# The first load of a streaming log-sum-exp, cut into four transfers of strided partitions ahead of the opening barrier

## The chip, the cores and the metric

The kernel runs on one core of one Trainium2 chip. The metric is the device time of one execution in microseconds (us), the median of several runs; less is better. All runs compared here were at a granted clock of 1.0. Differences below about 0.2% are within the noise unless an interval is given.

## The reference, cut to what matters

```
x: float32, 32 x 512 x 1024, standard normal
x_max = max(x, axis=-1)
out   = x_max + log(sum(exp(x - x_max), axis=-1))      # 32 x 512 values
```

The input is 64 MiB and is read once. The kernel leaves out the maximum, which these inputs don't need.

## The kernel before

Each of the 128 SBUF partitions owns 128 consecutive rows of the input. A row is 1024 float32 values, 4 KB, so the rows of neighbouring partitions lie 512 KB apart in memory. The rows come in 17 loads ("chunks") into a ring of 51 row slots. ScalarE (ACT) takes the exponentials in place; the sums are taken by VectorE (DVE) for some rows and by ACT's own accumulator for the others.

```python
CHUNKS = [(4, 1), (15, 11), (16, 10), (16, 15), (16, 0), (14, 0), ...]   # (rows, rows summed on DVE)
RING_ROWS = 51
FIRST_PARTS = [("sync", 0, 128)]
# ... cut ...
x_v = x_flat.rearrange("(p t) d -> p t d", p=P)

def load(i):
    (s, row), r = place[i], CHUNKS[i][0]
    # ... waits until the slots are free ...
    for engine, lo, hi in FIRST_PARTS if i == 0 else [("sync", 0, P)]:
        getattr(nc, engine).dma_start(
            out=ring[lo:hi, s : s + r], in_=x_v[lo:hi, row : row + r]
        ).then_inc(landed[i], 16)
# ... cut ...
load(0)
n_early = len(body.instructions)          # these go ahead of the opening barrier
# ... cut: for each chunk, load(i), then
nc.scalar.wait_ge(landed[i], 16 * (len(FIRST_PARTS) if i == 0 else 1))
# exp on ACT, sums on DVE or ACT ...
# ... cut: at the end the first n_early instructions are moved in front of
# the drain with which SyncE enters the opening barrier ...
```

So the first load, four rows for each partition (128 pieces of 16 KB, 2 MB), is issued by SyncE as its very first instruction (at 0.00 us), and the second load only after the barrier (at 0.78 us).

The softmax here doesn't subtract the row's maximum and nothing guards it: scores larger than these inputs give would overflow.

Of the kernel before, what the change touches and what calls it, by code (L numbers as in the profile page):

```python
# [1 line left out]

# [4 lines left out]



CHUNKS = [  # L10
    (4, 1), (15, 11), (16, 10), (16, 15), (16, 0), (14, 0), (12, 9), (9, 5), (7, 5), (5, 4),
    (4, 3), (3, 0), (2, 2), (2, 2), (1, 0), (1, 0), (1, 0),
]
RING_ROWS = 51

LN_AT = 5

FIRST_PARTS = [("sync", 0, 128)]


@with_exitstack
def kernel(
    ctx: ExitStack,
    tc: tile.TileContext,
    x: bass.AP,
    axis: bass.AP,
    out: bass.AP,
):
    nc = tc.nc
    P = nc.NUM_PARTITIONS  # L30

    assert axis in (-1, len(x.shape) - 1), f"only last-axis reduction supported, got {axis}"

    x_flat = x.flatten_outer_dims()
    N, D = x_flat.shape
    assert N % P == 0
    NB = N // P
    assert sum(r for r, _ in CHUNKS) == NB

    fp32 = mybir.dt.float32  # L40
    Exp = mybir.ActivationFunctionType.Exp
    Ln = mybir.ActivationFunctionType.Ln
    AX = mybir.AxisListType.X

    x_v = x_flat.rearrange("(p t) d -> p t d", p=P)
    out_v = bass.AP(tensor=out.tensor, offset=out.offset, ap=[[NB, P], [1, NB]])

    ring = nc.alloc_sbuf_tensor("ring", [P, RING_ROWS, D], fp32).ap()
    sums = nc.alloc_sbuf_tensor("sums", [P, NB], fp32).ap()
    res = nc.alloc_sbuf_tensor("res", [P, NB], fp32).ap()  # L50

    landed = [tc.alloc_semaphore(f"landed{i}") for i in range(len(CHUNKS))]
    act_done = tc.alloc_semaphore("act_done")
    dve_done = tc.alloc_semaphore("dve_done")
    stored = tc.alloc_semaphore("stored")


    hook = nc.pop_inst_callback()
    symbolic, nc._always_lower_symbolic_ap = nc._always_lower_symbolic_ap, False


    place = []
    row = slot = 0
    for r, _ in CHUNKS:
        if slot + r > RING_ROWS:
            slot = 0
        place.append((slot, row))
        slot += r
        row += r



    busy = [(0, 0)] * RING_ROWS
    acts = dves = 0

    def load(i):
        (s, row), r = place[i], CHUNKS[i][0]
        act_wait = max(a for a, _ in busy[s : s + r])
        dve_wait = max(d for _, d in busy[s : s + r])
        if dve_wait:  # L80
            nc.sync.wait_ge(dve_done, dve_wait)
        if act_wait:
            nc.sync.wait_ge(act_done, act_wait)
        for engine, lo, hi in FIRST_PARTS if i == 0 else [("sync", 0, P)]:
            getattr(nc, engine).dma_start(
                out=ring[lo:hi, s : s + r], in_=x_v[lo:hi, row : row + r]
            ).then_inc(landed[i], 16)

    def take_logs(lo, hi, dve_wait, act_wait):
        nonlocal acts  # L90
        nc.scalar.wait_ge(act_done, act_wait)
        nc.scalar.wait_ge(dve_done, dve_wait)
        nc.scalar.activation(out=res[:, lo:hi], in_=sums[:, lo:hi], func=Ln).then_inc(  # L93
            act_done, 1
        )
        acts += 1

    body = nc.main_func.blocks[-1]
    assert not body.instructions
    load(0)  # L100
    n_early = len(body.instructions)

    nc.scalar.preload_act_table_set("natural_log_exp_and_others")  # L103

    logged = 0
    done_before = [(0, 0)]
    for i, (r, n_dve) in enumerate(CHUNKS):
        if i:
            load(i)
        s, row = place[i]  # L110
        if i == LN_AT:
            logged = row
            take_logs(0, logged, *done_before[i])
        nc.scalar.wait_ge(landed[i], 16 * (len(FIRST_PARTS) if i == 0 else 1))
        if n_dve:
            nc.scalar.activation(  # L116
                out=ring[:, s : s + n_dve], in_=ring[:, s : s + n_dve], func=Exp
            ).then_inc(act_done, 1)
            acts += 1
            nc.vector.wait_ge(act_done, acts)  # L120
            nc.vector.reduce_sum(  # L121
                out=sums[:, row : row + n_dve], in_=ring[:, s : s + n_dve], axis=AX
            ).then_inc(dve_done, 1)
            dves += 1
            for j in range(n_dve):
                busy[s + j] = (0, dves)
        for j in range(n_dve, r):
            nc.scalar.activation(  # L128
                out=ring[:, s + j],
                in_=ring[:, s + j],  # L130
                func=Exp,
                accum_out=sums[:, row + j : row + j + 1],
            ).then_inc(act_done, 1)
            acts += 1
            busy[s + j] = (acts, 0)
        done_before.append((dves, acts))

    take_logs(logged, NB, dves, acts)
    nc.scalar.wait_ge(act_done, acts)
    nc.scalar.dma_start(out=out_v, in_=res).then_inc(stored, 16)  # L140
    nc.gpsimd.wait_ge(stored, 16)



    first = nc.main_func.blocks[0]
    head, work = first.instructions, body.instructions
    end = next(k for k, i in enumerate(head) if i.opcode == "UnconditionalBranch")
    head, tail = head[:end], head[end:]
    for ins in work[:n_early]:
        at = next(  # L150
            k for k, i in enumerate(head) if i.engine == ins.engine and i.opcode == "Drain"
        )
        head.insert(at, ins)
    first.instructions = head + work[n_early:] + tail
    body.instructions = []

    nc._always_lower_symbolic_ap = symbolic
    nc.push_inst_callback(hook)


# [1 line left out]
_INS = ['x', 'axis']  # L162
_OUTS = [((32, 512), 'float32')]

_NUMBERS = {'axis': -1}


# [26 lines left out]
```

## Time and profile before

| | before |
|---|---|
| median time | 164.12 us (164.01 to 164.53, 6 runs) |
| span of the profiled execution | 162.2 us |
| ACT first waits for data until | 7.42 us |
| second load awaited until | 25.62 us |
| fifth load awaited until | 83.69 us |

The profiled execution took 163.96 us, a little less than all six timed ones.

The following lines are the chain of waits of the kernel before: start in us, duration in us, what. It follows the work that ended last back from the end.

```profile
31 pieces in order of time: start us, us, what
0.71 0.07 issue
0.78 24.82 DMA ring<-in_x_dram
...
25.62 9.60 ACT ring L116
...
35.24 11.90 DVE sums L121
...
47.15 36.52 DMA ring<-in_x_dram
...
83.69 10.55 ACT ring L128 x21
...
159.36 0.25 ACT res L93
```

These are lines of its timeline: start, duration, engine, line, operation, operands, count, and in brackets how long the engine had been idle and what ended that.

```profile
0.00 2.38 SPq L85 DMA_DIRECT2D ring<-in_x_dram  x4
0.77 1.28 ACT L103 ACT_TABLE_LOAD   x1 [0.77 <-PEq L175]
7.42 1.06 ACT L116 ACTIVATE ring<-ring 128x1024 f32<-128x1024 f32 x1 [5.37 <-DMA ring<-in_x_dram]
25.62 9.59 ACT L116 ACTIVATE ring<-ring 128x11264 f32<-128x11264 f32 x1 [14.02 <-DMA ring<-in_x_dram]
44.98 8.74 ACT L116 ACTIVATE ring<-ring 128x10240 f32<-128x10240 f32 x1 [5.62 <-DMA ring<-in_x_dram]
83.69 1.06 ACT L128 ACTIVATE ring<-ring 128x1024 f32<-128x1024 f32 x1 [5.29 <-DMA ring<-in_x_dram]
```

Read together they say this. Up to 83.69 us ACT repeatedly waits for data; after it the chain stays with ACT. The chain names ACT and DVE between 25.6 and 47.2 us, because the issue of the fifth load waited for slots. But the records of single packets in the trace show that the engines were still moving the fourth load until about 64 us. The stream never stopped (the engines' mean busy share is 1.01 from 47 to 64 us, at 439 GB/s, and 0.97 from 64 to 83.6 us, at 421), so the landing at 83.67 us is plain transfer time. In this kernel, then, what delays the start of the stream should delay the end by as much.

The last view is the table of windows: window, its length, then for each engine its busy time and (number of instructions), the clock, the mean busy share of the 16 DMA engines, and GB/s.

```profile
core 0: us, DVE busy (x) ACT busy (x) POOL busy (x), PEclk, DMA share, GB/s
0.00:3.00 3.00, 0.00 (x0) 1.28 (x1) 0.20 (x4) 1.00 0.59 208
3.00:6.00 3.00, 0.00 (x0) 0.00 (x0) 0.00 (x0) 1.00 1.03 437
```

From 3 us on the first load runs at 437 GB/s, about what the loads after it reach (438 GB/s from 12 to 28 us). In the packet records each engine moves a 16 KB piece every 607 ns (27.0 GB/s).

### The profile page before, as it was taken

Reading aid. Unit: us, or ns where it says so; the run is one execution under the profiler, and the core shown is the slowest. Engines: PE = TensorE matmul, PEld = TensorE weight load, DVE = VectorE, ACT = ScalarE, POOL = GpSimd, SP = SyncE. Lnnn points to the kernel's source line nnn. Section 1 sums busy time; section 2 is a strip of 40 time slices with the busy share of each in tenths; the row PEclk is TensorE's granted clock in tenths of the full one; section 3 lists DMA queues with packets and bytes.
Section 4 is the critical chain, followed back from the end, with each engine's and each line's share of the span. In section 5 each row is a group of like instructions: output and inputs, shape, how many; then the busy total and the mean of one; then the engine's idle time right before and its main releaser. Section 6 shows DMA issues by size and latency. Waiting matters only on the chain.

```text
span 162.2 us, 213 instructions
## 1 busy us (share of the span) xinstructions
DVE 72.9 (45%) x11; ACT 124.1 (76%) x136; POOL 0.2 (0%) x4
## 2 busy tenths in 40 slices
DVE  0030000039960799000999900000006999799591
ACT  3180006997099971999339999999999999999993
POOL 0000000000000000000000000000000000000000
DMA  6999899969969959969988999999999999999970
GB/s 263 497 485 470 349 394 517 485 291 517 485 291 517 517 259 517 517 275 501 517 368 370 424 424 432 461 497 388 436 427 399 431 400 439 420 424 414 415 318 16
DMA packets 2593, 67.18 MB, mean 414 GB/s; under 512 B 288, under 2 KB 416, under 8 KB 800
## 3 DMA queue, kind: packets, MB, share of 16 engines
q1 hardware_dynamic: 2448, 67.11, 96.4%
q10 hardware_dynamic: 144, 0.07, 0.1%
q14 instruction: 1, 0.01, 0.0%
HBM read 67.11 MB, written 0.07 MB: 414 GB/s over the span
## 4 chain that ended last, share of the span: by engine, by line
ACT 52%; DMA 38%; DVE 7%; issue 1%
DMA ring<-in_x_dram 38%; ACT ring L128 30%; ACT ring L116 22%; DVE sums L121 7%; ACT res L93 0%
## 5 line engine op out<-in xcount | busy, mean ns | idle before, releaser
L121 DVE TENSOR_REDUCE sums<-ring 128x5 f32<-128x5120 f32 (+8 forms) x11 | 72.9, 6648 | 86.0 <-ACT ring L116 85.9
L116 ACT ACTIVATE ring<-ring 128x5120 f32<-128x5120 f32 (+8 forms) x11 | 59.3, 5394 | 29.4 <-DMA ring<-in_x_dram 29.4
L128 ACT ACTIVATE ring<-ring 128x1024 f32<-128x1024 f32 x61 | 63.4, 1041 | 5.3 <-DMA ring<-in_x_dram 5.3
L128 ACT ACTIVATION_READ_ACCUMULATOR ring<-ring 128x1 f32 x61 | 11.4, 187 | 0.0
L103 ACT ACT_TABLE_LOAD x1 | 1.3, 1283 | 0.8 <-PEq L175 0.8
L93 ACT ACTIVATE res<-sums 128x67 f32<-128x67 f32 (+1 forms) x2 | 0.5, 256 | 0.1
L175 POOL MEMSET const-bfloat16-1.0<- 128x1 bf16 x1 | 0.1, 101 | 0.0
L175 POOL MEMSET const-uint8-127<- 128x1 uint8 x1 | 0.1, 101 | 0.0
L175 POOL MEMSET const-float32-0.0<- 128x1 f32 x1 | 0.1, 98 | 0.2 <-issue 0.2
L175 POOL MEMSET const-float32-1.0<- 128x1 f32 x1 | 0.1, 98 | 0.0
## 6 DMA issues: line engine op xcount, KB each, us to landing
ring<-in_x_dram SPq DMA_DIRECT2D x1, 7680.0 KB, 24.8
ring<-in_x_dram SPq DMA_DIRECT2D x1, 7168.0 KB, 36.1
ring<-in_x_dram SPq DMA_DIRECT2D x1, 6144.0 KB, 21.6
ring<-in_x_dram SPq DMA_DIRECT2D x1, 4608.0 KB, 32.1
ring<-in_x_dram SPq DMA_DIRECT2D x2, 2048.0 KB, 26.3
ring<-in_x_dram SPq DMA_DIRECT2D x1, 3584.0 KB, 40.2
ring<-in_x_dram SPq DMA_DIRECT2D x1, 2560.0 KB, 44.4
ring<-in_x_dram SPq DMA_DIRECT2D x2, 1024.0 KB, 46.0
```

The lines of the kernel that those rows point to most:

```text
L93: nc.scalar.activation(out=res[:, lo:hi], in_=sums[:, lo:hi], func=Ln).then_inc(act_done, 1)
L103: nc.scalar.preload_act_table_set("natural_log_exp_and_others")
L116: nc.scalar.activation(out=ring[:, s : s + n_dve], in_=ring[:, s : s + n_dve], func=Exp).then_inc(act_done, 1)
L121: nc.vector.reduce_sum(out=sums[:, row : row + n_dve], in_=ring[:, s : s + n_dve], axis=AX).then_inc(dve_done, 1)
L128: nc.scalar.activation(out=ring[:, s + j], in_=ring[:, s + j], func=Exp, accum_out=sums[:, row + j : row + j + 1],).then_inc(act_done, 1)
L175: nc = _bacc.Bacc("TRN2", target_bir_lowering=False, num_devices=1)
```

## The change

The intent is to get the engines going earlier. The first load becomes four transfers of 16, 16, 32 and 64 partitions, taken in strides: on average one, one, two and four pieces for each of the 16 engines. The author hoped that the engines would start earlier on a first transfer of only 16 pieces. All four are issued ahead of the opening barrier.

```diff
-FIRST_PARTS = [("sync", 0, 128)]
+FIRST_PARTS = [(0, 8), (4, 8), (2, 4), (1, 2)]
...
-        for engine, lo, hi in FIRST_PARTS if i == 0 else [("sync", 0, P)]:
-            getattr(nc, engine).dma_start(
-                out=ring[lo:hi, s : s + r], in_=x_v[lo:hi, row : row + r]
+        for lo, step in FIRST_PARTS if i == 0 else [(0, 1)]:
+            nc.sync.dma_start(
+                out=ring[lo:P:step, s : s + r], in_=x_v[lo:P:step, row : row + r]
             ).then_inc(landed[i], 16)
```

## The prediction

> **What bounds the kernel now.** Until 83.67 us it is the stream of loads: the timeline and the chain of waits have the first load awaited until 7.42 us, the second until 25.62, the fifth until 83.67. The chain names a slot wait at 47.15, but the packet records show the engines still fed then (the fourth load drains at about 64 us), so the landing at 83.67 is pure transfer. From there to 159.6 us ScalarE (ACT) works almost without a gap. So what the first load gains or loses reaches the fifth landing and moves the end as much.
>
> **The first load now.** The timeline has its issue at 0.0 (372 ns on the queue). In the packet records the first packets start from 1.08 us, spread over almost 0.9 us among the 16 engines. Then each engine moves one 16 KB row every 607 ns (27.0 GB/s) without gaps; the eight rows end at 6.42 to 7.04 us, and that stagger of 0.6 us stays in every later load. The final store of 128 small rows spread its engines by only some 0.15 us[...].
>
> **What the change does.** The same 128 rows of 16 KB, in transfers of 16, 16, 32 and 64 rows. Added: three issues of about 330 to 370 ns on SyncE and 48 completion packets (9 ns each, three per engine). The later parts are issued at about 0.37, 0.7 and 1.05 us, before the engines finish the rows ahead, so no starvation. The opening barrier ends about 1.05 us later: the table load moves from 0.77 to 1.8 us, still long before the data; the second load is issued at about 1.8 instead of 0.78, with 5 us of packets ahead of it. Nothing lost there.
>
> Gain: [...] I estimate 0.1 to 0.4 us, from the two spreads above.
>
> [...]
>
> Weights: [...] first two parts only, about 165 (0.25); nearly all parts, 167 to 168.8 (0.4).
>
> **Prediction.** 165.2 us, range 163.7 to 168.6. Faster by over 2%: 0.01; within 2%: 0.68; slower: 0.31.
>
> **What would show it.** [...] The fifth landing moves from 83.67 by as much; ACT stays gapless after it. SyncE's four issues take about 0.35 us each before the barrier.
>
> **What would make it wrong.** [...] a completion write that stalls an engine between parts; a fixed cost per transfer above the 0.6 us of a row, which would starve the engines; a later load recovering a loss.

The danger was the assumption that, depending on the partitions which a transfer writes, a piece might take about 1.2 us, twice the 607 ns measured. Against the gain of 0.1 to 0.4 us the sum then had three cases: no piece slower, 163.6 to 164.2 us (weight 0.35); slow pieces in the first two parts, +1.2 us, about 165; slow pieces in nearly all parts, up to +4.9 us (0.6 us more for each of eight pieces) less what the stagger resolves, 167 to 168.8. The first load was to be awaited until about 7.1, 8.3 and up to 12 us. The point of 165.2 us and its range weigh all three cases.

## The result, and the profile after

| | before | after |
|---|---|---|
| median time, 6 runs each | 164.12 us (164.01 to 164.53) | 166.22 us (166.01 to 167.08) |
| ratio | | 1.0131, 95% interval 1.0109 to 1.0153 |
| first load awaited until | 7.42 us | 9.93 us |
| second load awaited until | 25.62 us | 28.07 us |
| fifth load awaited until | 83.69 us | 86.14 us |

A ratio here and below is the mean time of one kernel's runs over that of the other's in the same rounds, so it is not quite the ratio of the medians that are quoted.

The change costs 2.1 us, 1.3%: slower, clear of the noise, and within 2%. Lines of the timeline of the kernel after (columns as above):

```profile
0.00 4.99 SPq L85 DMA_DIRECT2D ring<-in_x_dram  x7
3.14 1.28 ACT L103 ACT_TABLE_LOAD   x1 [3.14 <-PEq L175]
9.93 1.06 ACT L116 ACTIVATE ring<-ring 128x1024 f32<-128x1024 f32 x1 [5.50 <-DMA ring<-in_x_dram]
28.07 9.59 ACT L116 ACTIVATE ring<-ring 128x11264 f32<-128x11264 f32 x1 [13.97 <-DMA ring<-in_x_dram]
47.42 8.74 ACT L116 ACTIVATE ring<-ring 128x10240 f32<-128x10240 f32 x1 [5.60 <-DMA ring<-in_x_dram]
86.14 1.06 ACT L128 ACTIVATE ring<-ring 128x1024 f32<-128x1024 f32 x1 [5.32 <-DMA ring<-in_x_dram]
103.76 1.06 ACT L128 ACTIVATE ring<-ring 128x1024 f32<-128x1024 f32 x1 [0.60 <-DMA ring<-in_x_dram]
```

The first wait ends 2.51 us later than before, and the three waits shown after it 2.44 to 2.45 us later (that for the fourth load, left out here, 2.42): everything is lost in the first 10 us, nothing more is lost and nothing recovered up to 86 us. The new wait of 0.60 us at 103.76 belongs to this one execution, which at 167.08 us was the longest of its six; a second profile of the same kernel, below, has no such wait. Because of it the chain of waits takes another way than before's, through the sixth load:

```profile
28 pieces in order of time: start us, us, what
...
3.53 43.87 DMA ring<-in_x_dram
...
47.42 8.75 ACT ring L116
...
56.19 10.83 DVE sums L121
...
67.04 36.69 DMA ring<-in_x_dram
...
103.76 14.65 ACT ring L128 x28
...
162.46 0.25 ACT res L93
```

The windows show where the transfer fell short:

```profile
core 0: us, DVE busy (x) ACT busy (x) POOL busy (x), PEclk, DMA share, GB/s
0.00:3.00 3.00, 0.00 (x0) 0.00 (x0) 0.20 (x4) 1.00 0.51 126
3.00:6.00 3.00, 0.00 (x0) 1.28 (x1) 0.00 (x0) 1.00 0.81 251
```

In the first 6 us before moved about 208 and 437 GB/s, after 126 and 251. The barrier also ends late (the table load on ACT starts at 3.14 us instead of 0.77), but the table is there at 4.42 us, 5.5 us before the first data.

The packet records of the first load show it in detail. Packets are ranked by their start; rank 1 to 16 is about the first piece of each engine, rank 17 to 32 the second.

| | before | after |
|---|---|---|
| SyncE's issues of the first load | 372 ns | 592, 571, 592, 594 ns |
| first packet starts | 1.08 us | 1.38 us |
| the first 16 packets start within | 0.89 us | 1.07 us |
| mean duration, ranks 1 to 16 | 921 ns | 1115 ns |
| ranks 17 to 32 | 628 ns | 886 ns |
| ranks 33 to 64 | 622 ns | 872 ns |
| ranks 65 to 128 | 613 ns | 620 ns |
| second load's first packet, slowest engine | 7.04 us | 9.58 us |

The engines start 0.3 us later, not earlier; the pieces of the first three transfers are slow, and those of the last are not. And the engines run dry: between about 3.0 and 4.8 us some of them have no packet at all, up to 9 of 16 at once, 0.47 us for each engine on average (0.25 us in the second profile, 0.02 us in the kernel before).

### The profile page after: what moved, and what is told of

Read it like the earlier page. It is cut to its first block, busy times and chain, and to the rows that moved or that the text cites. A ratio compares the mean times of both kernels' runs of the same rounds, so it can differ in the third digit from the quotient of the medians.

```text
span 165.3 us, 216 instructions
## 1 busy us (share of the span) xinstructions
DVE 72.9 (44%) x11; ACT 124.1 (75%) x136; POOL 0.2 (0%) x4
## 4 chain that ended last, share of the span: by engine, by line
DMA 49%; ACT 41%; DVE 7%; issue 0%; SPq 0%
DMA ring<-in_x_dram 49%; ACT ring L116 21%; ACT ring L128 19%; DVE sums L121 7%; SPq L85 0%; ACT res L93 0%
```

## The experiments

Three theories were set against each other.

- **Partitions.** The time of a piece depends on which partitions its transfer writes: those of the change's first two transfers (every eighth partition) and of neighbouring partitions are slow, those of every second partition are not. This was the assumption, which no trace of the kernel before shows; the halves test it.
- **Addresses of the reads** ("HBM theory"). The 16 rows that the change's first transfer reads lie 4 MB apart, and memory serves these worse. An assumption as well.
- **Cost** of each transfer: the issue, the late barrier, the completion.

A forecast that follows a cut and names no theory is the partition theory's: in thirds there are two, for pieces as fast as the halves' and for slow pieces in the first two parts; in after_tight and thirds_packed it is the one in which the time "stays". Its slow pieces are taken as twice as long: 1.2 us from 0.607, and in contig4 2.5 us from the 1.276 measured in halves_contig. These doublings are assumptions.

Twelve runs were made, in three groups, on two chips, each beside runs of before on the same chip. The edits are shown against the kernel after.

| run | first load | time, us | before beside it, us | ratio (95%) |
|---|---|---|---|---|
| again | the change, unedited | 166.35 | 164.30 | 1.0117 (1.0102 to 1.0131) |
| halves_strided | even, odd partitions | 164.59 | 164.30 | 1.0017 (1.0004 to 1.0030) |
| halves_contig | partitions 0-63, 64-127 | 168.98 | 164.30 | 1.0286 (1.0272 to 1.0300) |
| free4 | four cuts along the row | 164.47 | 164.30 | 1.0014 (0.9996 to 1.0032) |
| contig4 | sizes of the change, neighbouring partitions | 170.39 | 164.35 | 1.0369 (1.0355 to 1.0383) |
| src_packed | the change, input rows 512 KB apart | 165.54 | 164.35 | 1.0069 (1.0052 to 1.0086) |
| thirds | 32, 32, 64 partitions, strided | 165.08 | 164.35 | 1.0050 (1.0033 to 1.0067) |
| free2 | two cuts along the row | 164.36 | 164.35 | 1.0007 (0.9994 to 1.0019) |
| after_tight | the change, input rows 16 KB apart | 165.60 | 164.26 | 1.0080 (1.0061 to 1.0099) |
| before_tight | one transfer, input rows 16 KB apart | 164.46 | 164.26 | 1.0010 (0.9993 to 1.0026) |
| thirds_packed | thirds, input rows 512 KB apart | 165.28 | 164.26 | 1.0060 (1.0044 to 1.0077) |
| one_early | only the first part ahead of the barrier | 167.04 | 164.26 | 1.0157 (1.0131 to 1.0183) |

### again: the change once more

No edit.

> The changed kernel once more, unedited, because its profiled execution (167.08 us) was the longest of its runs and one engine's load lost 0.7 us near 100 us in it. All theories: about 1.3% over before, some 166.2 us. The profile should show which part of the loss is of every execution: the first load awaited until about 9.9 us (before: 7.4), the second until about 28.0 (25.6), the spread of the 16 engines' completions 1.5 us (0.7). If the four packets of 1.6 to 1.77 us in the third part come again, they belong to the change; if not, they are chance.

Measured: 166.35 us, and in the profile the same four waits end at 10.06, 28.20, 47.55 and 86.26 us, with none near 103.8:

```profile
10.06 1.06 ACT L116 ACTIVATE ring<-ring 128x1024 f32<-128x1024 f32 x1 [5.64 <-DMA ring<-in_x_dram]
28.20 9.59 ACT L116 ACTIVATE ring<-ring 128x11264 f32<-128x11264 f32 x1 [13.97 <-DMA ring<-in_x_dram]
47.55 8.74 ACT L116 ACTIVATE ring<-ring 128x10240 f32<-128x10240 f32 x1 [5.61 <-DMA ring<-in_x_dram]
86.26 1.06 ACT L128 ACTIVATE ring<-ring 128x1024 f32<-128x1024 f32 x1 [5.31 <-DMA ring<-in_x_dram]
```

The loss in the first load repeats (2.64 us) and goes through to the fifth. The slow second pieces come again (ranks 17 to 32: 1002 ns). The four packets of 1.6 to 1.77 us in the third part don't come again at that place; this profile has three of 1.3 to 1.5 us, which start at 4.08, 4.96 and 6.41 us.

### halves_strided and halves_contig: the same two transfers of 64, once in steps of two and once as neighbours

```diff
-FIRST_PARTS = [(0, 8), (4, 8), (2, 4), (1, 2)]
+FIRST_PARTS = [(0, 2), (1, 2)]                   # halves_strided

+FIRST_PARTS = [(0, 64), (64, 128)]               # halves_contig
-        for lo, step in FIRST_PARTS if i == 0 else [(0, 1)]:
+        for lo, hi in FIRST_PARTS if i == 0 else [(0, P)]:
-                out=ring[lo:P:step, s : s + r], in_=x_v[lo:P:step, row : row + r]
+                out=ring[lo:hi, s : s + r], in_=x_v[lo:hi, row : row + r]
```

> First load in two transfers, even and odd partitions (64 rows each[...]). [...] rows take 611 ns after the first and the time is within 0.3% of before, about 164.3 us. HBM theory [...] as slow as the change, about 166 us. Cost theory (the loss comes from the number of transfers and their issue, some 0.2 to 0.3 us more for a strided issue and a late barrier): a third of the loss, about 164.8 us.

> First load in two transfers, partitions 0 to 63 and 64 to 127 (64 rows each[...]). [...] each row about 1.2 us instead of 0.607, first load awaited until about 12 us less what the stagger resolves, time +3 to +4.9 us, 167 to 169 us. HBM theory: [...] about as before, 164.1 us. Cost theory: two transfers, so the same as the even and odd halves, about 164.5 us.

Measured: 164.59 and 168.98 us. As a pair they are as the partition theory had it and against both others (the 164.59 alone would not be far from the cost theory's 164.8). The two kernels have the same number of transfers, the same sizes and the same issue times (552 and 578 ns against 557 and 578 ns), and the first packets start at 1.34 and 1.35 us. In the packet records from the second piece of each engine on, the even and odd halves take 611 to 640 ns a piece (all but one). The contiguous halves take 1.1 to 1.29 us from the third piece on, most often 1.28. The windows of halves_contig show the same as a rate: where before moved 437 GB/s, this moves about half, for twice as long.

```profile
core 0: us, DVE busy (x) ACT busy (x) POOL busy (x), PEclk, DMA share, GB/s
0.00:3.00 3.00, 0.00 (x0) 1.16 (x1) 0.20 (x4) 1.00 0.69 175
3.00:6.00 3.00, 0.00 (x0) 0.12 (x1) 0.00 (x0) 1.00 1.00 208
6.00:9.00 3.00, 0.00 (x0) 0.00 (x0) 0.00 (x0) 1.00 1.08 229
```

The DMA engines are counted as busy all that time (share 1.00 and 1.08): the slow pieces look like busy engines here, not like idle ones.

The rows that are read change with the partitions here, so the reads are a rival. src_packed, below, answers it: its last transfer reads the same rows as the second half of halves_contig, but writes the odd partitions, and its pieces take mostly 611 ns. So what slows the contiguous halves is where they write.

The even and odd halves still lost 0.29 us. Their first packet starts 0.26 us later than before's, and their issue takes 552 ns instead of 372. That is of the size of the loss, which is itself hardly larger than the noise.

### free4 and free2: as many transfers, but every one over all partitions

```diff
-FIRST_PARTS = [(0, 8), (4, 8), (2, 4), (1, 2)]
+FIRST_PARTS = [(0, 1), (1, 2), (2, 3), (3, 4)]   # free4; free2: [(0, 1), (1, 4)]
-        for lo, step in FIRST_PARTS if i == 0 else [(0, 1)]:
+        for a, b in FIRST_PARTS if i == 0 else [(0, r)]:
-                out=ring[lo:P:step, s : s + r], in_=x_v[lo:P:step, row : row + r]
+                out=ring[:, s + a : s + b], in_=x_v[:, row + a : row + b]
```

> First load in four transfers too, but cut along the row: each carries one 4 KB row for all 128 partitions[...]. Four issues and the late barrier as in the change. [...] no slow packets (a 4 KB packet about 0.155 us), first load landed by 7.3 us, 163.9 to 164.3 us; perhaps a gain of 0.2 to 0.5 us, because the first packets are small and the stagger of 0.6 us between engines may shrink. Cost theory (four issues, barrier later): the loss of the change stays, 165.5 to 166.5 us. HBM theory: no statement beyond before, 164.1 us.

> First load in two transfers of all 128 partitions, one 4 KB row and then three. [...] each issue near 0.4 us, so nothing of the change's loss: 164.0 to 164.4 us. A small gain of 0.1 to 0.3 us over before is possible, as small first packets may start the engines closer together; nothing in the four-way cut along the row, which lost 0.14%, promises it.

Measured: 164.47 and 164.36 us, the same as before within the noise. Four issues ahead of the barrier (374, 424, 432, 432 ns here) and a table load at 2.20 us cost at most some 0.5 us by the interval. So the number of transfers and the late barrier are not the cause of the 2.05 us. The profile of free4 (an execution of 164.52 us) does have the first load awaited until 8.06 us and the fifth until 84.22, 0.64 and 0.53 later than the profile of before; the medians don't repeat that, and a few tenths of a us are not resolved here. The gain that I thought possible didn't come either. free2's first 16 packets start within 0.28 us of each other and its second load is awaited until 25.54 us (before: 25.62), but the fifth until 84.33, later than before's 83.69; nothing reached the end.

### contig4: the four sizes, of neighbouring partitions

```diff
+FIRST_PARTS = [(0, 16), (16, 32), (32, 64), (64, 128)]      # loop as in halves_contig
```

> The four sizes of the change (16, 16, 32, 64 rows) but of neighbouring partitions: 0-15, 16-31, 32-63, 64-127. [...] the first two rows of an engine take about 2.5 us each [...], the six others 1.28 us, about 12.6 us for the eight rows against 4.9: first load awaited until about 15 us, time about +7 us, 171 to 172 us. HBM theory (the loss comes from the 4 MB pitch of the engines' reads): [...] no worse than the contiguous halves and perhaps as before. Cost theory (number of transfers below 128 partitions, each issued in about 0.59 us): as the change, about 166.3 us.

Measured: 170.39 us, +6.0 instead of the +7 of the partition theory, and far from the other two. In the packet records nearly all pieces of the second transfer, of 16 neighbouring partitions, take 2.09 to 2.10 us, and those of the last two transfers, of 32 and 64, 1.15 to 1.29 us once the second has drained. But the first transfer's pieces, of 16 neighbouring partitions too, take only 0.8 to 1.7 us; why stays open. The direction and the order of size are the partition theory's, but the second transfer's pieces are shorter than the 2.5 us of its doubling. The issues here take 378 to 537 ns and the first packet starts at 1.00 us, earlier than in any strided transfer.

### src_packed and after_tight: the same partitions, other input addresses

Both give a wrong result: the first load reads other rows than it should. By calculation all outputs for such an input are close to 7.43, with a standard deviation of 0.04, so the comparison with the reference says nothing here.

```diff
+            n = P // step
+            at = 0 if i else {(0, 8): 0, (4, 8): 16, (2, 4): 32, (1, 2): 64}[(lo, step)]
-                out=ring[lo:P:step, s : s + r], in_=x_v[lo:P:step, row : row + r]
+                out=ring[lo:P:step, s : s + r], in_=x_v[at : at + n, row : row + r]     # src_packed
# after_tight: for i == 0 the source is tight[at : at + n], with
+    tight = x_flat[0 : 4 * P].rearrange("(p t) d -> p t d", p=P)
```

> WRONG RESULT on purpose. The four transfers of the change with the same SBUF partitions, but each reads neighbouring row groups of the input (0-15, 16-31, 32-63, 64-127), so that the pitch between the engines' reads is 0.5 MB in the first part instead of 4 MB. [...] SBUF partitions are what counts, so as the change, 166.0 to 166.6 us, rows of the first two parts near 0.9 to 1.2 us. HBM theory: the loss goes, about 164.6 us.

> WRONG RESULT on purpose. The four strided transfers of the change into the same SBUF partitions, but the first load reads one contiguous 2 MB block of the input (16 KB to a partition, 16 KB apart) instead of rows 512 KB apart. [...] the packed source, 512 KB apart, took 0.8 us of the 2.05 us away. [...] it stays: 165.3 to 165.7 us, rows of the first two parts still above 0.8 us. If it is still the addresses of the reads, it goes down to the 0.25 us of the even and odd halves: about 164.6 us.

Measured: 165.54 and 165.60 us. This is a miss for the partition theory alone: with nothing changed but the addresses of the reads, 0.7 to 0.9 us of the loss goes (1.19 and 1.34 us over before instead of 2.05). It is a miss for the address theory alone too: 1.2 to 1.3 us stay, however close the reads are. The second pieces are as slow as in the change (ranks 17 to 32: 1004 and 922 ns, against 886 and 1002 in its two profiles), so that slowness is not in the addresses of the reads. What the addresses do change visibly is the start: the first 16 packets start within 0.25 and 0.30 us, against 1.07 and 0.90. The packet records allow an account of the first load, in us, as means over the 16 engines:

| | before | the change (two profiles) | src_packed | after_tight |
|---|---|---|---|---|
| first piece starts at | 1.48 | 1.91, 1.84 | 1.48 | 1.49 |
| the eight pieces take together | 5.25 | 6.23, 6.23 | 6.30 | 6.48 |
| no packet after the start | 0.02 | 0.47, 0.25 | 0.11 | 0.21 |

So with other read addresses the pieces are no shorter. What goes is the late start, and the time without a packet shrinks (clearly in src_packed), though SyncE's issues are the same (592, 571, 592, 594 ns in the change, within 4 ns of it in both).

That fits the address theory in direction only: in the change's first transfer the 16 rows read lie 4 MB apart, in src_packed 512 KB, but the pieces themselves take 6.23 us together in the one and 6.30 in the other.

### before_tight: the tight source with one transfer

```diff
-FIRST_PARTS = [(0, 8), (4, 8), (2, 4), (1, 2)]
+FIRST_PARTS = [(0, 1)]                            # source tight, as above; result wrong on purpose
```

> WRONG RESULT on purpose. The kernel before, one transfer, but its first load reads one contiguous 2 MB block as in the run ahead of this one. If the slow first packets of before (0.6 to 1.36 us) and the spread of the engines' starts (0.9 us) come from the pitch of the reads, the first packets go together (spread below 0.4 us) and the time falls by 0.2 to 0.5 us, to about 163.9 us. If they are the start of the engines whatever is read, nothing changes: 164.2 to 164.4 us.

Measured: 164.46 us, no gain, and the first 16 packets still start within 0.86 us. In the kernel before, the addresses of the first load cost nothing that a denser source would give back. The address effect belongs to the cut.

### thirds and thirds_packed: the first two transfers joined

```diff
-FIRST_PARTS = [(0, 8), (4, 8), (2, 4), (1, 2)]
+FIRST_PARTS = [(0, 4), (2, 4), (1, 2)]            # thirds; thirds_packed also reads at : at + n
```

> Three transfers of 32, 32 and 64 rows: partitions 0, 4, ..., then 2, 6, ..., then the odd ones. [...] at the price of one issue less than the change. [...] rows 611 ns from the second on, about as the halves, 164.5 to 164.9 us. [...] up to +2.4 us less the stagger, about 165.5 to 166.5. Cost theory: three quarters of the loss of the change, about 165.7 us.

> WRONG RESULT on purpose. The three transfers (32, 32, 64 rows[...]) with neighbouring row groups of the input as their source. The three transfers lost 0.73 us. If the part above the halves' 0.25 us is the pitch of the reads, the time falls to 164.5 to 164.7 us; [...] it stays at 164.9 to 165.3 us.

Measured: 165.08 and 165.28 us. Joining the two 16-row transfers into one of every fourth partition takes back 1.3 of the 2.05 us. A packed source gives nothing further here. With packed sources the joining takes back next to nothing (1.02 us lost in thirds_packed, 1.19 in src_packed, and the intervals overlap), so the 1.3 us is not the price of the partitions alone. In the pieces the joining does show: in thirds_packed those of ranks 17 to 32 take 612 ns (1004 in src_packed, with the same 32 rows and the same 32 partitions) and those of the second transfer 611 to 636 ns but for one. So 32 partitions in steps of 4 have no slow pieces of their own in this run.

What is left, 0.73 and 1.02 us, is more than the halves' 0.29. The packet records put it in the last transfer: in thirds its first pieces take up to 1.85 us for about half of the engines, though the very same transfer of the odd partitions took 611 ns a piece in halves_strided. Why, these runs don't show; the trace doesn't say which engine moved a packet, and it stays open.

### one_early: only the first part ahead of the barrier

```diff
-    n_early = len(body.instructions)
+    n_early = 1
```

> The change with only its first part ahead of the opening barrier, the other three after it. The barrier then ends about 1.9 us earlier, and parts two to four are issued some 0.4 us later. If the late barrier costs anything (table load at 3.14 us, second load issued at 3.14), this is faster than the change by up to 0.5 us. If, as the trace says, nothing waits for it, it is the same as the change or up to 0.4 us slower, because the engines may run dry between the first and second part: 166.0 to 166.7 us.

Measured: 167.04 us, 0.7 us slower than the change in medians (another chip than again's) and above the range I had given. The second part is issued at 1.24 us instead of 0.65 and the fourth at 2.43 instead of 1.90. The run moves two things, an earlier barrier and later issues, so it doesn't separate them; it does show that on balance all parts ahead of the barrier was the better place. Its profile is of the fastest of its four runs (166.32 us) and has the waits where the change has them (first load 9.91, fifth 86.08); each engine is without a packet for 0.75 us on average, more than in the change (0.47 and 0.25).

## Why the prediction was right or wrong

The time (166.22 us) fell inside the range of 163.7 to 168.6, and the class, within 2%, was the likeliest one named. The point, 165.2, was 1.0 us too low. The range held because it spanned all three of the cases weighed; 166.22 lies in the gap between the second (about 165) and the third (167 to 168.8), so that it fell inside owes more to the width than to any one of them.

- **"What the first load gains or loses reaches the fifth landing and moves the end as much": right.** In the two profiles the first wait moved by 2.51 and 2.64 us, the fifth load's by 2.45 and 2.57. ACT stayed without gaps after it in the second profile, and that execution was 2.56 us longer than the profiled one of before.
- **"Gain ... 0.1 to 0.4 us": wrong in sign.** The first packet starts at 1.38 instead of 1.08 us. The start follows the end of the first issue by 0.79 us (before: 0.71), and that issue takes 592 ns rather than 372.
- **"Three issues of about 330 to 370 ns": wrong.** I took the duration of a 128-partition issue for a strided one. They took 571 to 594 ns (the first 592), and the barrier ended about 2.4 us later instead of 1.05. **"Before the engines finish the rows ahead, so no starvation": wrong.** The engines are without a packet for 0.47 and 0.25 us each in the two profiles. The issues are not the whole reason, since src_packed has the same ones and 0.11 us. **The late barrier itself: "nothing lost there" fits.** The table is there 5.5 us before the data, and free4, with a table load at 2.20 us, lost nothing clear of the noise.
- **The middle case's slow pieces (the first two about 1.2 us each instead of 0.607, +1.2 us): that pieces slow down with the partitions written is real, its share in the change is argued.** The halves show it by itself (+0.29 against +4.68 us). In the change the eight pieces of an engine take 0.98 us more together, near the +1.2, but not as foreseen: the second pieces take 0.89 to 1.00 us, slow but not doubled, and those of the third transfer, which takes every fourth partition, are slow too (ranks 33 to 64: 0.87 and 0.81 us).
- **Of my three weights the middle one, "first two parts only, about 165", named the right parts but not the time.** Its sum had the start as a gain and starvation as nothing; they were losses of 0.36 to 0.43 and 0.25 to 0.47 us on the mean engine. The first goes and the second shrinks when only the addresses of the reads are moved, which took 0.7 to 0.9 us off the time and had no term in the sum.

The loss can be laid out as a ladder, in which each rung cuts the transfer in front in two. One transfer: 0. Two (even, odd): +0.29 us, about the later start. Three (32, 32, 64): +0.73, where 0.44 sits in slow pieces of the last transfer, unexplained. Four (the change): +2.05, where the last cut, into two transfers of every eighth partition, costs 1.3 us. Of the 2.05 us about 0.8 also goes away when the reads are moved closer together, and then the last cut costs no more than the noise. How partitions and addresses divide the loss among them is not settled: the slow second pieces stay with packed reads, but the start recovers, and the time without packets in part.

## What to carry to other kernels

When a load is cut by partitions, look at which partitions each part takes before looking at its size: two cuts of 64 partitions cost 0.2% taken in steps of two and 2.9% taken as contiguous halves, with the DMA engines counted as busy in both. A cut along the row keeps all partitions in every transfer and cost nothing clear of the noise here (164.47 and 164.36 us), but even that gained nothing, since a smaller first transfer didn't bring the end of the first load forward (awaited until 8.06 us in free4 and 7.38 in free2, against 7.42). Before one spends effort on an earlier start, read from the packet records what the start waits for: here it followed the end of the issue by 0.71 us before and 0.79 after, and every partition cut in steps made the issue longer (508 to 594 ns, against 361 to 432 for all 128 partitions in a first load).
